# Two expert layers of a streaming encoder: x's place as a sixth weight buffer, and the shared expert's units spread over the middle blocks

## The chip, the cores and the metric

The kernel runs on one core of one Trainium2 chip. The metric is the device time of one execution in microseconds (us). Before the change the median of three runs is 1824.9 us (1823.75 to 1825.8). Times inside the kernel come from one profiled execution and are counted from its start.

## The reference

A residual trunk of two layers over 512 tokens of width 1024, all in float32. Layer 0 mixes tokens with a short gated convolution, layer 1 with gated DeltaNet linear attention. Each layer then has a mixture of experts: each token goes to the best of 8 groups and there to the best 2 of 8 experts, and a shared expert is added behind a sigmoid gate.

```python
x = x + gt1 * rmsnorm(mixer(h), norm_w[i, 1])
h = rmsnorm(x, norm_w[i, 2]) * (1.0 + sc2) + sh2
# each of 64 experts: hid = silu(xb @ w_gate[e]) * (xb @ w_up[e]); out = hid @ w_down[e]
# shared expert: ys = (silu(xt @ ws_gate) * (xt @ ws_up)) @ ws_down;  y = y + sigmoid(xt @ w_sg) * ys
x = x + gt2 * rmsnorm(y, norm_w[i, 3])
```

The residual x is 512 x 1024 words, 2 MB. Between the router's inputs and the last line nothing of the mixture of experts needs it. An expert's weights are 3 MB: 2 MB for gate and up, 1 MB for down. All 64 are loaded in each layer, 201 MB.

## The kernel before

*The ring.* All large weights go through a ring of five places in SBUF, each 128 partitions x 4096 words (2 MB). `load` (line 118) takes the next place and issues the DMA on SP's queue (lines 135 and 137). SP issues in program order: a load whose place is still being read holds up every load behind it. x has a place of its own of the same size (`new_x`).

*The blocks.* `moe` handles one layer's experts in 18 blocks, `ORDER = "QQ" + "QQPQQPQQPQQPQQQQ"`. A Q block has four experts with up to 32 tokens each, a P block two experts with up to 64. A Q block's gate and up weights take four places (`block_gu`: first the halves k < 4 of experts 0, 1 and 2, 3, then the halves k >= 4) and its down weights two (`block_dn`); a P block takes two and one. Block 0's down weights go to places outside the ring (y, hs, a `shw` buffer, part of xTb).

*One block on TensorE* (`blocks_in_order`, order written out by hand): gate-up products (line 1322, `gu`), then eight steps that alternate scatters of the block before (line 1379, `sca`, added to y by VectorE at line 1384) with gathers of a later block (line 1270, `gat`), the transposes of the hidden rows (line 1334), the down products (line 1357, `po`; for the last block line 1346, `pol`), and then, in some blocks, units of the shared expert. In the last block the scatters come ahead of the gate-up.

*The units.* Twelve per layer: eight of the shared expert's gate and up product (line 1408, `mix`), four of its down product (line 1431, `sda`). Each has a 512 KB load of its own into one of two `shw` buffers, in turn (lines 1416 and 1440). A block's unit loads are issued on SP between its gate-up and its down loads, and wait until the unit before the last has been computed. Line 1616 sets how many units a block has:

```python
n = 2 if b == NB - 2 else int(ne == 4 and not last and b > 1)
```

That is one in each of the blocks 2, 3, 5, 6, 8, 9, 11, 12, 14 and 15, and two in block 16. Behind block 16's units stands `gate_rows` (line 308, `gb`), which spreads the layer's last gate over the partitions.

*The end of a layer.* `down_last`, then `overflow`, a loop over experts with too many tokens (none here; its head at lines 1529 and 1530 is entered by all engines, and SP waits there for its loads), then the last block's scatters with the final norm and `x = x + ...` (`finish_chunk`).

*Ahead of the blocks.* `project_out` ends each mixer: per chunk of 128 tokens it adds to x (line 456), transposes x (line 544), multiplies by the router's weights (line 555) and scales x for the gathers (`front_split`, line 566). Its instructions and those of the DeltaNet mixer (`mixer1`) are put in order by a scheduler, apart from SP's.

*In `mixer1`* the decay's inputs are projected first (`project`, lines 383 to 385), transposed at line 712, worked through a chain of small VectorE instructions (lines 715 to 738, ending in `gg`), and summed by TensorE at lines 741 to 743.

Of the kernel before, what the change touches and what calls it, by code (L numbers as in the profile page):

```python
# [7 lines left out]
F32 = mybir.dt.float32  # L8
# [8 lines left out]
P = 128  # L17
T = 512
TC = T // P
D = 1024  # L20
# [18 lines left out]
ORDER = "QQ" + "QQPQQPQQPQQPQQQQ"  # L39
assert ORDER.count("P") == 4 and ORDER.count("Q") == 14  # L40
NB = len(ORDER)


def block_ranks():
# [71 lines left out]
class Trunk:  # L116
# [4 lines left out]
    def load(self, src, shape, place=None):  # L121
        n = int(np.prod(shape[1:]))
        assert n <= 4096
        if place is None:
            t = self.ring.tile([P, 4096], F32, name="ring")
        else:
            t = place.rearrange("p a b -> p (a b)")
        letters = "abcd"[:len(shape) - 1]
        v = t[:, :n]
        if len(shape) > 2:  # L130
            v = v.rearrange("p (%s) -> p %s" % (" ".join(letters), " ".join(letters)),
                            **{l: s for l, s in zip(letters, shape[1:])})
        if len(shape) == 4:
            for i in range(shape[1]):
                self.nc.sync.dma_start(out=v[:, i], in_=src[i])
        else:
            self.nc.sync.dma_start(out=v, in_=src)
        return v

    def run(self):  # L140
        nc, tc, A = self.nc, self.tc, self.A
        with tc.tile_pool(name="glob", bufs=1) as glob, \
                tc.tile_pool(name="ring", bufs=5) as ring, \
                tc.manual_schedule(engines={mybir.EngineType.SP}):
            self.glob, self.ring = glob, ring
            self.cst = glob.tile([P, C_END], F32, name="cst")
            self.ghi = glob.tile([P, K * T], F32R, name="ghi")
            self.glo = glob.tile([P, K * T], F32R, name="glo")
            self.col = glob.tile([P, W_END], F32, name="col")
            nc.scalar.dma_start(out=self.col, in_=A["cols"])  # L150
            nc.scalar.dma_start(out=self.cst, in_=A["consts"])
            self.ident = self.cst[:, C_ID:C_ID + P]
            self.new_x()
            for c in range(TC):
                nc.sync.dma_start(out=self.x[:, c], in_=A["x"][c * P:(c + 1) * P])
            self.bsu = glob.tile([P, P], BF16, name="bsu")
            nc.vector.tensor_copy(self.bsu, self.cst[:, C_SU:C_SU + P])
            self.bone = glob.tile([P, 1], BF16, name="bone")
            nc.vector.memset(self.bone, 1.0)
            tok = glob.tile([P, 2 * TC], F32, name="tok1")  # L160
            self.tok1, self.half = tok[:, :TC], tok[:, TC:]
            nc.scalar.dma_start(out=self.tok1, in_=A["tok1"])
            self.xsrc, self.xn = A["x"], None
            self.xs = tc.dram_tile([T, D], F32, name="xs")
            nc.vector.memset(self.half, -0.5)
            self.cs = glob.tile([P, K], F32, name="cs")
            nc.scalar.activation(self.cs, self.col[:, W_C:W_C + K], AF.Silu)
            self.gr = glob.tile([P, 512], F32, name="gr")
            self.mods = {}
            self.ada_tiles(0)  # L170
            self.ada_tiles(1)
            first = 0 if not self.only or min(self.only) < 2 else 1
            if self.only:
                with tc.tile_pool(name="ada0s", bufs=1) as sb, tc.tile_pool(name="ada0p", bufs=1, space=PSUM) as ps:
                    for f in self.ada_units(first, [0, 1, 2], sb, ps):
                        f()
            for n, step in enumerate((self.mixer0, lambda: self.moe(0), self.mixer1, lambda: self.moe(1))):
                if not self.only or n in self.only:
                    step()
                if self.upto == n + 1:  # L180
                    break
            if self.upto in (1, 2, 3):
                self.finish()
            self.drop_x()
# [215 lines left out]
    def project_out(self, wsrc, i, begun=None, shared=None):  # L400
# [4 lines left out]
        nc, tc = self.nc, self.tc  # L405
        front = not self.only or 2 * i + 1 in self.only
        with ExitStack() as cx:
# [41 lines left out]
            def post(c):  # L449


                parts = self.front_split(c - 1, sb) if front and c else iter(())
                next(parts, None)
                for s in halves:
                    x = self.x[:, c, s]
                    nc.vector.scalar_tensor_tensor(x, ts[c][:, s], st[c][:, 2:3], x, op0=ALU.mult, op1=ALU.add)
                    yield
                next(parts, None)
                yield
                if front:  # L460
                    yield from self.front_chunk(i, c, sb, ps)

            if shared or not begun:
                ws = w0 if shared else list(self.parts_of(w0, wp))
                for k in range(K):
                    for c in range(TC):
                        if k == 0:
                            tag, bufs = banks[0][c]
# [8 lines left out]
            for c in range(TC):  # L477
                tag, bufs = banks[1][c]
# [183 lines left out]
    def mixer1(self):  # L662
        nc, tc, A, cst = self.nc, self.tc, self.A, self.cst
# [4 lines left out]
        with ExitStack() as ctx:  # L668
            hhi, hlo = self.parts(K, T)
            with ExitStack() as cx:  # L670
# [101 lines left out]
                for h in range(H):  # L772
# [137 lines left out]
                    for j in range(4):  # L910
                        b = slice(32 * j, 32 * j + 32)
# [68 lines left out]

                if self.only:
                    wo = [self.load_out(A["gdn_out_w"], 0)]
                wo.append(self.load_out(A["gdn_out_w"], 1))
                sums = {c: ps.tile([P, T], F32, tag=("pj", "pj", "tp", "gq")[c], name="oacc", bufs=2 if c < 2 else 1)
                        for c in range(TC)}
                yhi, ylo = self.parts(TC, K, P)
                for k in range(K):
                    self.split_y(yT, [k])
                    whi = wp.tile([P, T], F32R, name="whi")
                    wlo = wp.tile([P, T], F32R, name="wlo")  # L990
                    act(whi, wo[0][:, k], AF.Copy)
                    nc.gpsimd.tensor_tensor(out=wlo, in0=wo[0][:, k], in1=r32(whi), op=ALU.subtract)
                    for c in range(TC):
                        self.mm3(sums[c], yhi[:, c, k], ylo[:, c, k], whi, wlo, k == 0, k == K - 1)
            self.project_out(A["gdn_out_w"], 1, begun=(wo, sums))

    def places(self, sb, tag, words, bufs=2):
# [447 lines left out]
    def moe(self, i):  # L1445
# [3 lines left out]
        with ExitStack() as ctx:  # L1449
# [16 lines left out]
            xA, _ = self.pair(sb)  # L1466
            xB, late = self.pair(sb)
            hw = yp[0].tile([P, D], F32, name="shw")
            src, gu = self.block_gu(i, 0, None)

            dn = self.block_dn(i, src, [self.y, hs.rearrange("p (k a) t -> p k (a t)", k=2), hw,
# [131 lines left out]
    def blocks_in_order(self, i, m, rt, rp, pairs, hs, shw, sb, ps, units, columns, scatter):  # L1603

        nc = self.nc
        xT, nxt, oh = pairs
        for b in range(1, NB):
            last = b == NB - 1  # L1610
            src, gu = self.block_gu(i, b, rt)
            ne = len(src)
            if b % 2 == 0:
                xT = nxt
            h = P * (b % 2)
            n = 2 if b == NB - 2 else int(ne == 4 and not last and b > 1)
            now = [u() for u in units[:n]]
            units = units[n:]
            dn = self.block_dn(i, src)
            adds = [(c, h) for h in range(2) for c in range(TC)]  # L1620
            if last:
                for a in adds:
                    scatter(*a)
                adds = []
            hid = self.gate_up_hid(sb, ps, [x[:, h:h + P] for x in xT], ne, gu)
            steps = iter(())
            if b < NB - 2:
                if b % 2 == 0:
                    oh = self.slot_onehot(sb, rt["slot"], P * (b + 2), 256)
                    nxt, _ = self.pair(sb)  # L1630
                steps = self.gather(ps, m, oh, nxt, (2, 3) if b % 2 else (0, 1))
            elif not last:
                steps = self.route_over(rt, rp, sb, ps)
            for n in range(8):
                if adds:
                    scatter(*adds.pop(0))
                if n == (0 if last else 5):
                    hT = self.turn(sb, ps, hid)
                next(steps, None)
            for _ in steps:  # L1640
                pass
            if not last:
                scatter = self.rows_out(sb, ps, self.down_mm(ps, hT, ne, dn), *columns(b))
            for u in now:
                u()
            if b == NB - 2:
                gt = self.gate_rows(shw, ps, 1, ("shw", "mix"))

        assert not units
        po = self.down_last(ps, hT, ne, dn)  # L1650
        self.overflow(i, m, rt, hs, sb, ps)
        if i == 0 and not self.only:
            nc.scalar.dma_start(out=hs[:, 0], in_=self.A["rows"][1])
        self.down(sb, ps, hT, ne, dn, *columns(NB - 1), self.finish_chunk(i, gt, sb, ps), False, po)
# [116 lines left out]
```

## Time and profile before

| | us |
|---|---|
| median of three runs (lowest to highest) | 1824.9 (1823.75 to 1825.8) |
| the profiled execution, its own time | 1825.65 |
| its span (first to last instruction) | 1823.8 |
| TensorE matmul busy | 1616.1 (89%) |
| VectorE busy | 852.8 (47%) |
| ScalarE busy | 479.1 (26%) |
| GpSimd busy | 175.6 (10%) |
| moved by DMA | 523.17 MB, mean 287 GB/s |

The page divides the span into 40 slices of 45.6 us and gives for each what the DMA engines moved. A busy TensorE is not one at its peak: matmuls overlap, and one that waits for its data can count as idle or run at a lower granted clock. So the stages are read one by one below: the expert blocks of layer 0 lie between 288 and 802 us, those of layer 1 between 1302 us and the end, and the DeltaNet mixer between them.

### The profile page before, as it was taken

How to read it: one execution, taken by the hardware profiler on the slowest of the kernel's cores; microseconds unless marked ns; L12 is line 12 of the kernel's file. 1: busy time of each engine (PE TensorE's matmuls, PEld its weight loads, DVE VectorE, ACT ScalarE, POOL GpSimd, SP SyncE). 2: the span in 40 equal slices, each digit the busy share in tenths (PEclk: the TensorE clock that was granted, in tenths of full speed). 3: DMA queues.
4: the chain of work that ended last, by engine and by line, in shares of the span. 5: the costliest groups of instructions: out<-in, count | busy, mean ns of one | idle time of the engine just before them, and what ended most of it. 6: DMA issues, size and time to landing. Idle time of an engine off the chain costs nothing. (4 is left out here: it accounts for less than half of the span.)

```text
span 1823.8 us, 27772 instructions
## 1 busy us (share of the span) xinstructions
PE 1616.1 (89%) x11102; PEld 985.6 (54%) x11102; DVE 852.8 (47%) x1761; ACT 479.1 (26%) x978; POOL 175.6 (10%) x160
## 2 busy tenths in 40 slices
PE   6999977899999998868998999998689999989985
PEld 3777755445445454426676766656444545445542
DVE  1886454434334342445666666625543424334335
ACT  4222351211111110034344434415231111111101
POOL 1000110000000000024323323310000000000001
PEclk8999987999999999988999999999699999999997
DMA  9873426999999999786111111116589999999992
GB/s 402 353 304 124 202 108 250 376 419 418 420 417 411 419 419 419 292 353 244 62 59 59 59 59 59 53 59 271 208 336 420 416 419 418 419 419 415 420 399 93
DMA packets 71511, 523.17 MB, mean 287 GB/s; under 512 B 8340, under 2 KB 8532, under 8 KB 16852
## 3 DMA queue, kind: packets, MB, share of 16 engines
q1 hardware_dynamic: 67684, 511.02, 68.6%
q10 hardware_dynamic: 3696, 10.34, 1.6%
q8 instruction: 89, 1.46, 0.3%
q14 instruction: 42, 0.34, 0.0%
HBM read 517.11 MB, written 4.23 MB: 286 GB/s over the span
## 5 line engine op out<-in xcount | busy, mean ns | idle before, releaser
L1384 DVE TENSOR_TENSOR y<-y,sca 128x512 f32<-128x512 f32 x272 | 186.0, 686 | 97.3 <-PE sca L1379 96.4
L1322 PE MATMUL gu<-ring,xTb 128*32 128x512 f32 (+1 forms) x1024 | 170.6, 634 | 31.8 <-DMA ring<-in_moe_gu 31.8
L1270 PE MATMUL gat<-ohg,ghi 128*128 128x256 f32 x576 | 162.6, 304 | 32.1 <-DVE ohg L1245 10.8
L1326 DVE TENSOR_TENSOR hid<-hid,gu 128x256 f32<-128x256 f32 x36 | 15.2, 421 | 311.0 <-ACT hid L1325 311.0
L1270 PE MATMUL gat<-ohg,glo 128*128 128x256 f32 x576 | 154.7, 291 | 0.0
L1270 PEld LDWEIGHTS gat<-ohg,ghi 128*128 128x128 f32 x576 | 113.8, 198 | 61.4 <-ACT xTb L1276 17.4
L1379 PE MATMUL sca<-ohi,G 128*128 128x512 f32 x288 | 126.4, 439 | 15.6 <-DVE y L1382 5.4
L1322 PE MATMUL gu<-ring,xTa 128*32 128x512 f32 (+1 forms) x1024 | 134.6, 610 | 0.2
L1322 PEld LDWEIGHTS gu<-ring,xTb 128*32 128x32 f32 (+1 forms) x1024 | 47.3, 119 | 147.1 <-issue 82.9
L1379 PE MATMUL sca<-olo,G 128*128 128x512 f32 x288 | 118.5, 411 | 0.0
L1270 PEld LDWEIGHTS gat<-ohg,glo 128*128 128x128 f32 x576 | 114.1, 198 | 7.9
L1357 PE MATMUL po<-ring,hT 128*32 128x512 f32 (+1 forms) x896 | 118.1, 602 | 0.0
L1682 POOL TENSOR_TENSOR ft<-y,gt 128x512 f32<-128x512 f32 x8 | 12.4, 1550 | 1058.9 <-DVE y L1384 1058.1
L1408 PE MATMUL mix<-h2T,shw 128*128 128x512 f32 x256 | 114.1, 599 | 0.0
L385 PE MATMUL pj<-ghi,wlo 128*128 128x512 f32 x264 | 113.4, 430 | 0.2 <-POOL wlo L681 0.2
L383 PE MATMUL pj<-ghi,whi 128*128 128x512 f32 x264 | 110.3, 418 | 1.6 <-DVE xh L789 0.8
L1325 ACT ACTIVATE hid<-gu 128x256 f32<-128x256 f32 x36 | 13.9, 385 | 357.8 <-PE gu L1322 357.8
L384 PE MATMUL pj<-glo,whi 128*128 128x512 f32 x264 | 107.8, 408 | 0.0
L681 POOL TENSOR_TENSOR wlo<-ring,whi 128x512 fp32r<-128x512 f32 x66 | 86.1, 1305 | 184.7 <-ACT whi L680 125.1
L1372 DVE SCALAR_TENSOR_TENSOR olo<-po,tab_s,ohi 128x512 fp32r<-128x512 f32 x68 | 51.1, 751 | 96.6 <-ACT ohi L1371 96.6
L1379 PEld LDWEIGHTS sca<-ohi,G 128*128 128x128 f32 x288 | 56.1, 195 | 62.8 <-issue 31.1
L1322 PEld LDWEIGHTS gu<-ring,xTa 128*32 128x32 f32 (+1 forms) x1024 | 36.6, 115 | 88.5 <-issue 88.2
(402 smaller groups left out, 2781.7 us busy)
## 6 DMA issues: line engine op xcount, KB each, us to landing
ring<-in_moe_gu SPq DMA_DIRECT2D x256, 1024.0 KB, 14.5
ring<-in_moe_w_down SPq DMA_DIRECT2D x120, 1024.0 KB, 13.2
ring<-in_ada_w SPq DMA_DIRECT2D x24, 2048.0 KB, 10.8
ring<-in_gdn_w SPq DMA_DIRECT2D x8, 2048.0 KB, 12.3
ring<-in_conv_in_w SPq DMA_DIRECT2D x8, 1536.0 KB, 11.8
shw<-in_shared_gu SPq DMA_DIRECT2D x16, 512.0 KB, 15.4
x<-in_x SPq DMA_DIRECT2D x8, 512.0 KB, 6.3
ring<-in_conv_out_w SPq DMA_DIRECT2D x2, 2048.0 KB
```

The lines of the kernel that those rows point to most:

```text
L383: mm(out, ah, bh, start=first, stop=False)
L384: mm(out, ah, bl, start=False, stop=False)
L385: mm(out, al, bh, start=False, stop=last)
L681: nc.gpsimd.tensor_tensor(out=wlo, in0=w[:, k:k + 4], in1=r32(whi), op=ALU.subtract)
L1270: nc.tensor.matmul(g[:, kk], part[:, c, k], oh[:, c], start=(kk + c + lo == 0), stop=(kk + lo == 2 and c == TC - 1), skip_group_check=True)
L1322: nc.tensor.matmul(gu[s * j:s * j + s], xT[k][:, s * j:s * j + s], pieces(j, k), start=(k == 0), stop=(k == K - 1), skip_group_check=True)
L1326: nc.vector.tensor_tensor(out=hid, in0=hid, in1=gu[:, 256:512], op=ALU.mult)
L1357: self.nc.tensor.matmul(po[h][s * j:s * j + s], hT[:, k, s * j:s * j + s], pieces(j, k)[:, 512 * h:512 * h + 512], start=(k == 0), stop=(k ...
L1372: nc.vector.scalar_tensor_tensor(lo, po[h], gcol, r32(hi), op0=ALU.mult, op1=ALU.subtract)
L1379: nc.tensor.matmul(sc, G[:, c * P:(c + 1) * P], part, start=(n == 0), stop=(n == 1))
L1384: nc.vector.tensor_tensor(out=ys, in0=ys, in1=sc, op=ALU.add)
L1408: nc.tensor.matmul(acc, w[:, k], self.h2T[:, k], start=(k == 0), stop=(k == K - 1))
```

## The change

x's residual is copied to a DRAM tile `xk` chunk by chunk as `project_out` completes it. While the blocks run, x's place stands at the end of the list of ring places, so the ring has six. After the last block's loads it leaves the list, and x is read back from `xk` on SP's queue, ahead of `down_last`. A table `UNITS` names the blocks of the twelve units: blocks 5 and 9 get two, block 16 none; `gate_rows` moves from block 16 to block 15. The ring's places are now taken from a list in place of a rotating pool; `gdn_out_w`'s second load is written behind the products that read the first.

```diff
+UNITS = (2, 3, 5, 5, 6, 8, 9, 9, 11, 12, 14, 15)
+assert all(ORDER[b] == "Q" for b in UNITS)
...
         if place is None:
-            t = self.ring.tile([P, 4096], F32, name="ring")
+            t = self.pieces.pop(0)
+            self.pieces.append(t)
...
-                tc.tile_pool(name="ring", bufs=5) as ring, \
+                tc.tile_pool(name="ring", bufs=1) as ring, \
...
+            self.pieces = [ring.tile([P, 4096], F32, name="ring%d" % n) for n in range(5)]
...
+            self.xk = tc.dram_tile([T, D], F32, name="xk")
...
+                if front:
+                    nc.scalar.dma_start(out=self.xk[c * P:(c + 1) * P], in_=self.x[:, c])
                 next(parts, None)
...
-                wo.append(self.load_out(A["gdn_out_w"], 1))
                 sums = {c: ps.tile([P, T], F32, tag=("pj", "pj", "tp", "gq")[c], name="oacc", bufs=2 if c < 2 else 1)
...
                         self.mm3(sums[c], yhi[:, c, k], ylo[:, c, k], whi, wlo, k == 0, k == K - 1)
+                wo.append(self.load_out(A["gdn_out_w"], 1))
...
+            if not self.only:
+                self.xplace = self.x.rearrange("p c d -> p (c d)")
+                self.pieces.append(self.xplace)
             src, gu = self.block_gu(i, 0, None)
...
-            n = 2 if b == NB - 2 else int(ne == 4 and not last and b > 1)
+            n = UNITS.count(b)
...
-            if b == NB - 2:
+            if b == NB - 3:
                 gt = self.gate_rows(shw, ps, 1, ("shw", "mix"))
         assert not units
+        if not self.only:
+            self.pieces = [p for p in self.pieces if p is not self.xplace]
+            for c in range(TC):
+                nc.sync.dma_start(out=self.x[:, c], in_=self.xk[c * P:(c + 1) * P])
         po = self.down_last(ps, hT, ne, dn)
```

**SP, block 16 of layer 0, before** (rows of `in_moe_gu` and `in_moe_w_down` are the ring's loads, one expert's half or a whole down matrix each):

```order
L135 ISA
L135 DMA ring<-in_moe_gu 128x2048
L1440 DMA shw<-in_shared_w_down 128x1024 x2
L135 ISA
L135 DMA ring<-in_moe_w_down 128x2048
```

**SP, block 5 of layer 0, now** (line numbers are now those of the changed kernel):

```order
L139 DMA ring_63<-in_moe_gu 128x2048
L1426 DMA shw<-in_shared_gu 128x1024 x2
L139 ISA
L139 DMA x<-in_moe_w_down 128x2048
```

The two unit loads in one block stand in block 5 (and likewise in block 9), between its gate-up and its down loads; in block 16 none stands there. x's place is written by expert loads, here a down matrix.

**SP, the end of layer 0's blocks, now:**

```order
L139 DMA ring_67<-in_moe_w_down 128x2048
L139 ISA
L139 DMA ring_67<-in_moe_w_down 128x2048
L1668 DMA x<-xk 128x1024 x4
L1543 TENSOR_LOAD oid
```

Before, the last down load was followed by the loop's head (L1529 TENSOR_LOAD oid) directly; now x's four loads stand between them.

**TensorE, the head of the DeltaNet mixer, before** (`pj` is the projection, `tp<-cst,th` the transposes of the decay's inputs, `tp<-gg,cst` the first use of the decay):

```order
L384 MATMUL pj<-glo,whi 128x512
L712 MATMUL tp<-cst,th 128x16 x4
L385 MATMUL pj<-ghi,wlo 128x512
...
L385 MATMUL pj<-ghi,wlo 128x512
L741 MATMUL tp<-gg,cst 128x32
L742 MATMUL tp<-gg,cst 128x32
L743 MATMUL tp<-gg,cst 128x32
```

**The same place now:**

```order
L393 MATMUL pj<-ghi,wlo 128x512
L722 MATMUL tp<-cst,th 128x16 x4
L391 MATMUL pj<-ghi,whi 128x512
L751 MATMUL tp<-gg,cst 128x32
L752 MATMUL tp<-gg,cst 128x32
L753 MATMUL tp<-gg,cst 128x32
```

Between the transposes and the first use stood 19 projections; now one stands there, and the others follow later.

## Rows read from the trace of the kernel before

**Rows 1.** The page's 40 slices of the span: GB/s moved in each.

```profile
GB/s 402 353 304 124 202 108 250 376 419 418 420 417 411 419 419 419 292 353 244 62 59 59 59 59 59 53 59 271 208 336 420 416 419 418 419 419 415 420 399 93
```

**Rows 2.** Windows: stretch, length, busy time by engine, clock, DMA share, GB/s.

```profile
282.00:294.00 12.00, 10.41 (x63) 6.32 (x62) 2.52 (x13) 2.04 (x4) 0.00 (x0) 0.70 0.00 1
...
322.00:761.30 439.30, 404.91 (x2348) 209.57 (x2340) 163.32 (x292) 73.42 (x137) 0.00 (x0) 0.98 1.01 416
761.30:775.50 14.20, 11.87 (x65) 4.44 (x68) 6.02 (x10) 1.20 (x2) 0.00 (x0) 1.00 0.02 10
775.50:781.50 6.00, 4.25 (x36) 1.04 (x28) 0.42 (x1) 0.77 (x2) 0.00 (x0) 1.00 0.90 350
...
1337.00:1776.50 439.50, 403.47 (x2342) 210.14 (x2334) 164.20 (x294) 73.36 (x137) 0.00 (x0) 0.98 1.01 416
```

**Rows 3.** Windows of layer 0's blocks 4 (P), 5 and 6 (Q, one unit).

```profile
405.25:424.74 19.49, 18.85 (x99) 10.32 (x99) 6.92 (x11) 2.81 (x6) 0.00 (x0) 1.00 1.01 418
424.74:451.42 26.68, 26.04 (x165) 13.67 (x163) 12.58 (x23) 5.56 (x10) 0.00 (x0) 1.00 1.02 418
451.42:484.30 32.88, 29.65 (x164) 13.56 (x163) 7.74 (x12) 4.79 (x9) 0.00 (x0) 0.95 1.01 419
```

**Rows 4.** Timeline of TensorE, block 6: start, us, instruction, idle before and releaser.

```profile
459.54 5.32 PE L1322 MATMUL gu<-ring,xTb 128*32 128x512 f32 x26 [1.46 <-DMA ring<-in_moe_gu]
...
477.23 7.13 PE L1408 MATMUL mix<-h2T,shw 128*128 128x512 f32 x16
```

**Rows 5.** Timeline of TensorE, layer 0, blocks 16 and 17.

```profile
740.13 3.64 PE L1357 MATMUL po<-ring,hT 128*32 128x512 f32 x32
743.70 3.72 PE L1431 MATMUL sda<-shw,hs 128*128 128x256 f32 x16
...
762.46 1.12 PE L308 MATMUL gb<-gr,cst 64*128 64x512 f32 x2 [0.97 <-DVE y L1435]
...
765.32 0.50 PE L1379 MATMUL sca<-ohi,G 128*128 128x512 f32 x1
...
771.11 3.64 PE L1322 MATMUL gu<-ring,xTa 128*32 128x512 f32 x32
774.57 3.62 PE L1322 MATMUL gu<-ring,xTb 128*32 128x512 f32 x32
...
782.17 3.62 PE L1346 MATMUL pol<-ring,hT 128*32 128x512 f32 x26 [0.99 <-DMA ring<-in_moe_w_down]
787.55 0.47 PE L1379 MATMUL sca<-ohi,G 128*128 128x512 f32 x1 [1.76 <-ACT ohi L1371]
```

**Rows 6.** Timeline of SP, layer 0, loads of blocks 16 and 17.

```profile
710.75 7.78 SPq L1440 DMA_DIRECT2D shw<-in_shared_w_down  x2
...
744.92 30.72 SPq L135 DMA_DIRECT2D ring<-in_moe_w_down  x4
```

**Rows 7.** Timeline of all engines, layer 0, end of project_out.

```profile
260.69 1.94 PE L544 MATMUL ftp<-cst,x 128*128 128x128 f32 x8 [4.41 <-issue]
...
262.47 3.69 PE L555 MATMUL flp<-wr,h2T 128*128 128x73 f32 x16
...
264.09 2.19 ACT L566 ACTIVATE xnf<-x,rx 128x1024 f32<-128x1024 f32 x1 [1.67 <-POOL rx L552]
```

**Rows 8.** The page's DMA issues: count, size of one, median us to landing.

```profile
ring<-in_moe_gu SPq DMA_DIRECT2D x256, 1024.0 KB, 14.5
...
xs<-x ACTq DMA_DIRECT2D x4, 512.0 KB, 13.0
x<-xs SPq DMA_DIRECT2D x4, 512.0 KB, 3.6
```

**Rows 9.** Timeline of TensorE, layer 1, first scatter behind the overflow loop.

```profile
1802.96 0.47 PE L1379 MATMUL sca<-ohi,G 128*128 128x512 f32 x1 [1.80 <-ACT ohi L1371]
```

**Rows 10.** Timeline of TensorE, head of the DeltaNet mixer.

```profile
840.04 0.42 PE L712 MATMUL tp<-cst,th 16*128 16x16 f32 x4
...
847.11 0.38 PE L741 MATMUL tp<-gg,cst 128*128 128x32 f32 x2 [2.03 <-DVE gg L738]
```

More of the change, by code (lines that the diff above doesn't have):

```diff
@@ L142, in run @@
         with tc.tile_pool(name="glob", bufs=1) as glob, \
-                tc.tile_pool(name="ring", bufs=5) as ring, \
+                tc.tile_pool(name="ring", bufs=1) as ring, \
                 tc.manual_schedule(engines={mybir.EngineType.SP}):
-            self.glob, self.ring = glob, ring
+            self.glob = glob
+            self.pieces = [ring.tile([P, 4096], F32, name="ring%d" % n) for n in range(5)]
             self.cst = glob.tile([P, C_END], F32, name="cst")
```

## The prediction

> **What bounds the kernel now.** Read first the 40 slices of the page [rows 1]: the GB/s line stands at 411 to 420 twice, in slices 9 to 16 and again from 31 to 38. These are the expert blocks of the two layers, which stream their weights. The windows of layer 0 [rows 2] show how the stretch begins and ends. The ring is full and nothing moves from 282 to 294 us (1 GB/s). From 322 to 761.3 us the DMA share is 1.01, at 416 GB/s over 439.3 us. Then it is idle again up to 775.5 (10 GB/s), and one last piece of 2.1 MB comes until 781.5. Layer 1 repeats this: 439.5 us at 416 GB/s, ending at 1776.5.
>
> So in the middle the stream is the bound, and the blocks show with how much to spare [rows 3]: the P block 4 takes TensorE 19.49 us, the Q block 5, with one unit of the shared expert, 26.68. A Q block loads twelve times 1.05 MB, 30.2 us at 416 GB/s, a P block half, 15.1, and a unit's 0.52 MB 1.3. TensorE gains on the stream in Q blocks and loses on it in P blocks; where it is ahead, it waits inside the gate-up products. Block 6 shows it [rows 4]: 1.46 us for `in_moe_gu`, and the 26 products behind that take 5.32 us. The last row is a unit: 7.13 us. A Q block without one is thus 26.68 - 7.13 = 19.55 us.
>
> The end is another matter [rows 5]. Block 16's down product begins at 740.13. Behind it stand two units of the shared expert's down product, 743.70 to 762.46 (9.4 us each), then the gate's rows to 765.32, then block 16's scatters, and only at 771.11 block 17's gate-up, whose weights ended with the stream at 761.3. One piece is missing even then: block 17's second down piece finds no free place. SP's own timeline has its four down loads begin at 744.92 and take 30.72 us to issue [rows 6]; the place comes free when half the gate-up is read, at 774.57, and the last 26 down products start at 782.17 after a 0.99 us wait for `in_moe_w_down`. The first scatter behind the overflow loop starts at 787.55. So from 761.3 on the order of work and the five places bound the kernel, not the bandwidth.
>
> **The change, part by part.** *The sixth place.* The load that before waited at 282 finds x's place and moves 2.1 MB, 5.0 us at 416 GB/s, in a stretch that was idle [rows 2]. From 294 on the four places freed by block 0 fill as before, but they now hold what comes after. The stream that starts at 322 has 2.1 MB less ahead of it, just block 17's last piece: the same 439 us now bring all weights by 761.3.
>
> *Does the place come in time?* x's last chunk is complete when its transposes start, at 260.69, and its copy to DRAM can be issued then; ScalarE's scaling reads it last, from 264.09 to 266.3 [rows 7]. The copy's landing is not in this trace; nearest is `xs<-x`, the same size and queue, 13.0 us (median) to land [rows 8]: 273.7, still before 282. Bounds: free at 266.3 or at 273.7, no cost in either. The copies' 2.1 MB lie in slices at 108 and 271 GB/s [rows 1], with room. ScalarE issues the last copy while it would wait for the transposes anyway; the order also puts the h2T copy ahead of the square, and the router's products, which end at 266.2, are later than both [rows 7]: I take 0, with ends of -0.5 and +2 for both layers.
>
> *The units.* Two down units and the gate's rows leave the end. Blocks 5 and 9 get a second unit, the others move up. Sums of TensorE against the stream, from the durations above: blocks 5 to 9, four Q, one P and six units, 4 x 19.55 + 19.49 + 6 x 7.13 = 140.5 us against 4 x 30.2 + 15.1 + 6 x 1.3 = 143.7; blocks 10 to 13, 92.3 against 93.1; blocks 14 to 16, 3 x 19.55 + 2 x 9.4 + 2.9 = 80.4 against 93.2. TensorE is faster in each, barely in the first two. So the units cost nothing as long as the ring covers the local ups and downs; six places hold 12.6 MB, 30 us of stream. If that cover is short, the stream stops. Followed load by load (5.0 us a piece; a place is free when the product that reads it ends), the tightest is block 11's second down piece, with 1 to 2 us left. So I charge 1 us per layer, with ends of 0 and 6 (nearly a unit).
>
> *The end now.* Weights end at 761.3. Before, the last piece ended near 781.4 and its products started at 782.17: 0.8 us. So the last 26 down products start at 762.1. Their time is bounded by two rows of 26 products, 3.62 us [rows 5] and 5.32 behind a wait [rows 4]. I take 5.3, since block 17 must now wait for its gate-up and its down weights: 767.4. From there to the first scatter 1.76 us, as before: 769.2. That is 787.55 - 769.2 = 18.3 us less.
>
> Here a rule speaks against the change. The rows show that products behind a short wait took 5.32 us instead of 3.62, at a granted clock that fell from 1.00 to 0.95 over the block [rows 3, 4]. The Trainium skill, page "TensorE: Matmul & The Clock Gate", section "HAM oscillation — how this bites in real kernels", says that a burst that has waited for its DMA restarts with the clock throttled, every time; by it all 26 products run at the lower of the two levels, 1.2 GHz. Twice 3.62 is 7.2 us, which makes the end 3.8 us later over two layers than the sum below; 3.62 would make it 3.4 earlier.
>
> *x comes back.* The loop behind the down products is entered by all engines, and SP, which issues the reload last, waits there for its landing. x's 2.1 MB follow the weights: 761.3 + 5.0 + 0.8 = 767.1, just under the 767.4 of TensorE. I take 0; `x<-xs`, 3.6 us for one of four [rows 8], leaves an upper end of 3 us per layer.
>
> *Layer 1*, by the same steps [rows 9]: 1776.5 + 0.8 + 5.3 + 1.8 = 1784.4 against 1802.96: 18.6 us.
>
> *What the scheduler moved.* In the DeltaNet mixer 19 projections stood between the transposes of the decay (L712) and their use (L741); now one does, as the order shows. VectorE's chain between the two lasts from 840.46 to 847.11, 6.65 us, and TensorE waited 2.03 of it [rows 10]. Now it waits 6.65 - 0.24 = 6.4, and the 18 products have to be made later: +4.4 us. Ends: 0, if TensorE would have waited later anyway; 8, if the products after the longer wait start slow. `gdn_out_w`'s second load is only written later; on SP it stands where it stood: 0.
>
> *Sum.* 18.3 + 18.6 - 2 - 4.4 = 30.5 us less than the profiled execution's 1825.65 (span 1823.8): **1795**. The median of the runs, 1824.9, lies 0.75 lower, inside the rounding here.
>
> **Rivals.**
> (a) *The ring runs full around the double units.* For it: 140.5 against 143.7 leaves 3 us in 140. Against it: the median gate-up load lands 14.5 us after its issue [rows 8], 12 of them queue. Price: 5 to 8 us per layer more, so 1805 to 1811. Chance 0.18.
> (b) *x's place comes late*, so that the sixth place does not help the fill. For it: landings of 13.0 us. Against: it would have to land 8.3 us later than that. Price: the 5.0 us per layer again, 1805. Chance 0.05.
> (c) *No slow products and no mixer stall*: 30.5 + 3.4 + 4.4, so 1787. Chance 0.10.
> (d) *All products behind block 17's waits are slow*, as the rule above has it: 7.2 us each, 1795 + 3.8 = 1799. For it: the wait of block 6 was shorter than those of block 17 will be, some 4 us. Against: block 6's 26 were slow only in part. Chance 0.12.
> (e) *SP's order turns against it: slower.* A unit's tile has two buffers, so block 6's unit load waits until block 5's first unit is done, and block 9's second until block 8's; behind them in SP's queue stand all later loads. The last places of a block's gate-up come free at its end; from there to the unit's end are 19.55 - 7.1 + 7.1 = 19.5 us (a gate-up takes 7.1, 771.11 to 778.2 [rows 5]), and the two freed places carry 10. If nothing else is queued the stream stops 9.5 us, four times over both layers: 38 us, giving 1833. For it: the same wait is there before, SP's two unit loads of block 16 begin at 710.75 and take 7.78 us [rows 6]. Against: the stream stayed at full rate through that one, and it decides only from a backlog under 9.5 us, where the rows give 12. Chance 0.05.
>
> **How the numbers follow.** My forecast, 1795, has 0.47, and 0.03 is left for a change that nets out. Faster by over 0.2% (3.6 us, about what a measurement of this kernel can tell from no change): forecast and (a) to (d), 0.92. Within it: 0.03. Slower: (e), 0.05. The range is 1786 to 1812: it takes in (c) and all of (a), the ends of the mixer and of x's reload with them, and leaves out the slower case.
>
> **What would show it.** Right: DMA share near 1 from 322 to 761 without a hole at blocks 6 and 9 to 12; about 5 us more of transfer between 282 and 294; no `sda` product in block 16; block 17's gate-up near 750, with a wait for `in_moe_gu`; the first scatter behind the loop near 769; a wait of about 6 us on `gg` in the mixer. Wrong: a hole in the stream behind a double unit, SP waiting on a unit with the DMA idle, or engines waiting for x at the loop.

## The result, and the profile after

The changed kernel takes 1794.2 us (median of four runs, 1791.25 to 1797.47) against 1825.35 before: ratio 0.9831, 95% interval 0.9813 to 0.985, 1.7% faster. The forecast was 1795. Its profiled execution is the slowest of the four, 1797.47 with a span of 1795.6.

First the page of the changed kernel: the granted clock, DMA share and GB/s of its 40 slices (44.9 us each).

```profile
PEclk8999987999999999977999999979699999999987
DMA  9874447899999999967211111108489999999995
GB/s 400 334 291 177 185 170 308 365 419 420 419 418 408 418 419 419 413 255 289 81 60 60 60 60 60 54 7 362 183 343 418 419 419 419 419 411 419 419 419 222
```

The two plateaus of [rows 1] are there, and each ends earlier. The windows of the changed kernel show their two edges and block 11 (columns as in [rows 2]):

```profile
278.00:290.00 12.00, 10.41 (x65) 6.28 (x64) 2.52 (x13) 2.04 (x4) 0.00 (x0) 0.72 0.41 170
322.00:755.00 433.00, 403.08 (x2398) 210.63 (x2397) 169.64 (x303) 75.06 (x141) 0.00 (x0) 0.99 1.01 418
755.00:762.00 7.00, 3.91 (x26) 0.90 (x30) 0.00 (x0) 0.27 (x1) 0.00 (x0) 1.00 1.00 404
...
581.66:609.46 27.80, 26.19 (x181) 15.86 (x179) 13.36 (x24) 5.57 (x10) 0.00 (x0) 1.00 0.99 403
```

The stretch that moved 1 GB/s [rows 2], here 4 us earlier, moves 170 GB/s, 2.04 MB: the sixth piece. From 322 the DMA share is 1.01 for 433 us, and only block 11 dips a little (403 GB/s). Now TensorE at the end of layer 0 (before: [rows 5]):

```profile
742.89 0.62 PE L1332 MATMUL gu<-ring,xTa 128*32 128x512 f32 x2
...
749.79 3.62 PE L1332 MATMUL gu<-ring,xTb 128*32 128x512 f32 x26 [1.45 <-DMA ring<-in_moe_gu]
...
757.27 1.04 PE L1356 MATMUL pol<-ring,hT 128*32 128x512 f32 x2 [0.89 <-DMA ring<-in_moe_w_down]
760.19 3.62 PE L1356 MATMUL pol<-ring,hT 128*32 128x512 f32 x26 [1.88 <-DMA ring<-in_moe_w_down]
766.78 0.79 PE L1389 MATMUL sca<-ohi,G 128*128 128x512 f32 x1 [2.97 <-ACT ohi L1381]
```

No unit stands behind block 16, and block 17's gate-up starts 28.2 us earlier. It waits for its weights, as do the down products: the stream is the bound up to the end. The last 26 products take 3.62 us, but the scatter waits 2.97 us where it waited 1.76 before. The DeltaNet mixer's head on TensorE (before: [rows 10]):

```profile
817.30 0.42 PE L722 MATMUL tp<-cst,th 16*128 16x16 f32 x4 [0.68 <-ACT th L719]
819.26 0.49 PE L391 MATMUL pj<-ghi,whi 128*128 128x512 f32 x1 [1.55 <-ACT whi L690]
826.46 0.61 PE L751 MATMUL tp<-gg,cst 128*128 128x32 f32 x2 [6.70 <-DVE gg L748]
...
829.43 0.80 PE L393 MATMUL pj<-ghi,wlo 128*128 128x512 f32 x1
830.02 0.63 PE L391 MATMUL pj<-ghi,whi 128*128 128x512 f32 x1
...
834.51 0.40 PE L393 MATMUL pj<-ghi,wlo 128*128 128x512 f32 x1
```

The wait is 6.70 us, and the projections behind it start every 0.43 us until 834, then every 0.23. In the kernel before, too, they start every 0.43 us behind its wait of 2.03, from 849 to 852.5.

For the sum, the span is cut at four starts of instructions on TensorE: block 0's gate-up, and the first scatter behind the loop, in both layers. All kernels of this study, in us of their profiled executions; each ratio is to the kernel before as measured beside that run on the same chip (1824.0 to 1825.6):

| kernel | to block 0 | layer 0's blocks | mixer | layer 1's blocks | tail | median, ratio to before |
|---|---|---|---|---|---|---|
| before | 288.45 | 499.1 | 515.1 | 500.3 | 20.8 | 1825.35 |
| after | 284.64 | 482.1 | 525.0 | 481.4 | 22.4 | 1794.2, 0.9831 |
| sixth_only | 283.92 | 491.3 | 529.1 | 490.0 | 20.9 | 1816.1, 0.9953 |
| units_only | 286.95 | 492.6 | 514.8 | 495.0 | 20.8 | 1811.5, 0.9937 |
| list_only | 289.92 | | 525.4 | | | 2089.4, 1.1455 (another computation, below) |
| copy_only | 284.65 | 499.5 | 514.8 | 499.1 | 21.5 | 1823.9, 1.0003 |
| units_early | 290.02 | 505.8 | 529.6 | 505.1 | 21.2 | 1843.8, 1.0089 |
| pool_ring | 289.91 | 482.6 | 508.7 | 481.2 | 22.4 | 1786.6, 0.979 |
| pool_behind | 290.07 | 482.7 | 515.6 | 480.5 | 20.8 | 1787.4, 0.9788 |
| pool_last | 285.79 | 483.7 | 514.2 | 480.3 | 21.1 | 1783.8, 0.9771 |
| after_again | 284.15 | 482.7 | 528.7 | 481.3 | 22.4 | 1798.2, 0.9847 |

The change gains 17.0 and 18.9 us in the blocks and 3.8 ahead of them, and gives back 9.9 in the mixer and 1.6 in the tail: 28.2 us of span. The block columns repeat within 1.6 us for the same blocks. The first and the mixer column don't: units_early and the changed kernel have the same code up to block 0 and differ by 5.4 us there; in the window 82 to 92 us, inside that difference, their granted clocks are 0.62 and 0.83. So only differences of 6 us or more, or rows, count in these two columns.

### The profile page after: what moved, and what is told of

It reads as the page before. It is cut to its first block, busy times and chain, and to the rows that moved or that the text cites. A ratio compares the mean times of both kernels' runs of the same rounds, so it can differ in the third digit from the quotient of the medians.

```text
span 1795.6 us, 27951 instructions
## 1 busy us (share of the span) xinstructions
PE 1602.0 (89%) x11102; PEld 985.9 (55%) x11102; DVE 853.3 (48%) x1761; ACT 478.1 (27%) x978; POOL 176.4 (10%) x160
## 4 chain that ended last, share of the span: by engine, by line
PE 67%; DMA 12%; DVE 11%; ACT 4%; issue 3%; POOL 2%; SPq 0%; ACTq 0%; POOLq 0%; DVEq 0%
PE gu L1332 11%; PE gat L1280 7%; PE po L1367 6%; PE sca L1389 6%; DMA ring<-in_moe_gu 6%; PE mix L1418 5%; PE acc L391 4%; PE acc L392 4%; PE acc L393 4%; PE sda L1441 3%; DMA ring<-in_moe_w_down 3%; PE pj L393 2%; PE pj L391 2%; PE pj L392 2%; DMA x<-xk 2%
## 5 line engine op out<-in xcount | busy, mean ns | idle before, releaser
L1332 PE MATMUL gu<-ring,xTb 128*32 128x512 f32 (+1 forms) x960 | 128.9, 607 | 9.7 <-DMA ring<-in_moe_gu 9.7
L1701 POOL TENSOR_TENSOR ft<-y,gt 128x512 f32<-128x512 f32 x8 | 12.4, 1552 | 1024.0 <-DVE y L1394 1023.2
L1332 PEld LDWEIGHTS gu<-ring,xTb 128*32 128x32 f32 (+1 forms) x960 | 36.7, 114 | 94.8 <-issue 73.3
L1418 PEld LDWEIGHTS mix<-h2T,shw 128*128 128x128 f32 x256 | 47.3, 190 | 69.7 <-issue 62.0
## 6 DMA issues: line engine op xcount, KB each, us to landing
ring<-in_ada_w SPq DMA_DIRECT2D x24, 2048.0 KB, 12.4
ring<-in_conv_in_w SPq DMA_DIRECT2D x8, 1536.0 KB, 18.9
```

Source lines behind the costliest of these rows:

```text
L1332: nc.tensor.matmul(gu[s * j:s * j + s], xT[k][:, s * j:s * j + s], pieces(j, k), start=(k == 0), stop=(k == K - 1), skip_group_check=True)
L1418: nc.tensor.matmul(acc, w[:, k], self.h2T[:, k], start=(k == 0), stop=(k == K - 1))
```

## The experiments

**The parts of the gain.** *sixth_only* is the changed kernel with the old places of the units:

```diff
-            n = UNITS.count(b)
+            n = 2 if b == NB - 2 else int(ne == 4 and not last and b > 1)
...
-            if b == NB - 3:
+            if b == NB - 2:
```

> Only the sixth place (with the copy, the reload and the list); the twelve units as before, two in block 16. Theory: every weight after block 5's down load comes 5.0 us earlier, so block 16 starts 5 us earlier, and the last piece no longer waits for block 17's gate-up (1 to 2 us more): 6 to 7 us less per layer at the first scatter behind the loop (before: 787.55), 12 to 14 in all; the list's order of the DeltaNet mixer takes 9.9 back, the front of layer 0 gives 0 to 4: 1818 to 1823. Rival: block 16's two units bind the end whatever the weights do, so the gain is only the last piece's 1 to 2 us per layer: 1830 or more.

*units_only* is the kernel before with the table and `gate_rows` in block 15, the reverse of these lines.

> Only the table of units; five places from the rotating pool, no copy of x. Theory: five places are too few for the double units in blocks 5 and 9, the stream stops there for some us and the last piece still comes late: first scatter near 779, some 8 us less per layer, total near 1810; holes in the stream in blocks 6 to 12. Rival: five places carry them too, only the 5.0 us of the last piece are missing at the end: first scatter near 772, 15 us less per layer, total near 1797; DMA share 1.0 throughout.

sixth_only: ratio 0.9953 (0.9939 to 0.9967), 7.8 and 10.3 us less in the blocks. That is more than the 6 to 7 of the theory (the total of 1816.1 lies 2 us below its 1818 to 1823) and far from the rival's 1 to 2. Its end shows what is left: the units, then all 32 down products in one run, at full clock and behind no weights.

```profile
746.54 3.72 PE L1441 MATMUL sda<-shw,hs 128*128 128x256 f32 x16 [0.97 <-DVE y L1445]
...
769.77 3.64 PE L1356 MATMUL pol<-ring,hT 128*32 128x512 f32 x32 [0.47 <-ACT hT L1346]
```

units_only: 0.9937 (0.9919 to 0.9955), 6.5 and 5.4 us less in the blocks; the total is near the 1810 of the theory (which had 8 per layer) and far from the rival's 15 and 1797. Two rows of its windows and two of its TensorE timeline say why:

```profile
569.16:588.61 19.45, 18.81 (x99) 10.28 (x98) 6.92 (x11) 2.81 (x6) 0.00 (x0) 1.00 0.83 334
588.61:616.39 27.78, 26.17 (x180) 15.86 (x178) 13.37 (x24) 5.56 (x10) 0.00 (x0) 1.00 0.95 393
```

```profile
761.85 4.13 PE L1325 MATMUL gu<-ring,xTb 128*32 128x512 f32 x32
...
772.32 5.40 PE L1349 MATMUL pol<-ring,hT 128*32 128x512 f32 x26 [0.56 <-DMA ring<-in_moe_w_down]
```

With five places blocks 10 and 11, behind block 9's two units, run the stream at shares of 0.83 and 0.95 against 1.01 elsewhere, some 5 us lost, and the last piece still waits until block 17's gate-up has freed a place at 761.85. So each part alone leaves the other's bound standing, order of work or places: the two alone add up to 14.3 and 15.7 us, together they bring 17.0 and 18.9.

**When are units hidden?** *units_early* doubles all units of the changed kernel:

```diff
-UNITS = (2, 3, 5, 5, 6, 8, 9, 9, 11, 12, 14, 15)
+UNITS = (2, 2, 3, 3, 5, 5, 6, 6, 8, 8, 9, 9)
```

> The changed kernel with all twelve units in six double ones: blocks 2, 3, 5, 6, 8 and 9. Theory: a unit is hidden only while TensorE's blocks are no longer than the loads they free; blocks 2 to 9 then take 6 x 19.55 + 2 x 19.49 + 8 x 7.13 + 4 x 9.4 = 251 us against 227 us of stream, so the ring runs full, SP waits for units with nothing queued, and the lost transfer is not made up behind it: 20 us more per layer, near 1834, with holes in the stream between 455 and 605. Rival: the layer's sum of TensorE is below the stream's, and what is lost early is won back late: 1794 to 1800.

1843.8, ratio 1.0089 (1.0062 to 1.0115): 23.6 and 23.7 us more in the blocks than after, where the theory had 20, and far from the rival's total of 1800 at most. Its windows by block (5, 8, 9 and 10) and SP's wait:

```profile
433.00:467.00 34.00, 32.67 (x182) 15.76 (x178) 12.58 (x23) 5.98 (x11) 0.00 (x0) 1.00 0.87 356
...
521.00:558.00 37.00, 33.45 (x214) 21.73 (x210) 12.31 (x23) 5.51 (x10) 0.00 (x0) 1.00 0.77 312
558.00:595.00 37.00, 33.45 (x211) 21.73 (x210) 14.58 (x29) 4.18 (x8) 0.00 (x0) 1.00 0.98 405
595.00:614.00 19.00, 18.36 (x97) 10.32 (x98) 7.11 (x12) 2.81 (x6) 0.00 (x0) 1.00 0.84 346
```

```profile
SPq L1426 <- PE mix L1418: 75.0, 8, 14.9
```

The holes are where the theory puts them, and the later blocks, stream-bound again, don't win them back. This is what rivals (a) and (e) describe, made to happen; how much of it is the full ring and how much SP's waits for units, this run doesn't separate. In the changed kernel the same row of SP reads

```profile
SPq L1426 <- PE mix L1418: 37.9, 4, 9.6
...
SPq L1544 <- DMA x<-xk: 14.8, 6, 8.7
```

The four waits of rival (e) are there, up to 9.6 us, but the queue ahead of them lasted. Block 5's stretch keeps a share of 1.01:

```profile
417.82:452.16 34.34, 33.01 (x180) 15.85 (x179) 12.58 (x23) 6.16 (x11) 0.00 (x0) 1.00 1.01 418
```

**What the mixer lost.** *list_only* is the kernel before with the list of five places in place of the pool.

```diff
-            t = self.ring.tile([P, 4096], F32, name="ring")
+            t = self.pieces.pop(0)
+            self.pieces.append(t)
```

> Only the ring's list in place of the pool, five places, with the second output load written behind the products; no copy, units as before. Theory: this alone makes the DeltaNet mixer's wait of 6.7 us and the slow projections behind it, 9.9 us more between the loop of layer 0 and block 0 of layer 1; nothing else changes: 1833 to 1836. Rival: the mixer's 9.9 come from the copies or the other changes, or the early end of layer 0: then 1825, or with the 3.8 us that layer 0's front won, 1831.

A Q block has six loads: with five fixed places its second down load takes the place of its first gate-up piece, whose products then read down weights. So its experts are another computation (the gate-up waits 252.5 us for `in_moe_w_down`), its total of 2089.4 says nothing of the 1833 to 1836 expected, and only the mixer is read from it: 525.4 us, as in the changed kernel, with a wait of 6.69 us for `gg`. Every kernel with the list has 525 to 530 us in that column, every one with the pool 509 to 516.

*copy_only* adds only the copies and the reload to the kernel before.

> Only the copy of x to DRAM and its reload ahead of the last down products; five places from the pool, units as before. Theory: the copies cost nothing, the reload follows the last piece (781.5 before) and lands some 6 to 7 us later, near 788, while the last products end at 785.8: the loop is held 1 to 3 us per layer, 1827 to 1831. Rival: the reload's landing is hidden and the front's order moves nothing: 1825; or the front gives its 3.8 us through the copy: 1822.

Ratio 1.0003 (0.9986 to 1.0021): the theory's 1827 to 1831 did not come, though its mechanism did. The mixer stays at 514.8. The loop opens 2.97 us behind the last products, as after, so the reload holds it by 1.2 us; the fronts give that back (below).

*pool_ring* keeps the pool outside the expert blocks and the list of six inside:

```diff
-            t = self.pieces.pop(0)
-            self.pieces.append(t)
+            if self.pieces is None:
+                t = self.ring.tile([P, 4096], F32, name="ring")
+            else:
+                t = self.pieces.pop(0)
+                self.pieces.append(t)
...
-                self.pieces.append(self.xplace)
+                self.pieces = [self.ring.tile([P, 4096], F32, name="ring") for n in range(5)] + [self.xplace]
```

> The change, but the ring's places come from the rotating pool outside the expert blocks, and from the list of six (five of the pool's and x's) only inside them; the second output load stands where it stood before the change. Theory: the list alone moved the projections of the DeltaNet mixer; with 19 of them back between the decay's transposes and its use, the wait falls from 6.7 to 2.0 us, the slow projections behind it go, and the 9.9 us come back: near 1784.5, the blocks as in the changed kernel. Rival: the mixer's loss comes from what the early end of layer 0 leaves behind, not from the order: 1792 to 1796.

1786.6, ratio 0.979 (0.9767 to 0.9813), near the 1784.5 of the theory. The wait at the decay's first use is again that of [rows 10]:

```profile
831.98 0.38 PE L752 MATMUL tp<-gg,cst 128*128 128x32 f32 x2 [2.03 <-DVE gg L749]
```

So the list, not the copies and not the shorter layer 0, moved the projections. (Both runs move `gdn_out_w`'s second load together with the list; which of the two edits the scheduler answered to was not separated.) The slow projections behind the wait did not go, as expected here: they start every 0.43 us up to 837.1, as in the kernel before.

**What the reload costs.** *pool_behind* reads x back behind `self.overflow(...)` in both layers, *pool_last* only in layer 1:

```diff
+        if i and not self.only:
+            for c in range(TC):
+                nc.sync.dma_start(out=self.x[:, c], in_=self.xk[c * P:(c + 1) * P])
```

> The same, and x is read back behind the loop for overflowing experts instead of ahead of the last down products. Theory: in the changed kernel the loop waits for x, which lands 5.08 us behind the last weight, while the last 26 products take 3.62: 1.2 us per layer, and the scatters behind the longer wait run at the lower clock (1.6 us in layer 1). Without it the time from the last product to the first scatter is 1.8 us again instead of 2.97, total 2.4 to 4 us less than with the reload ahead, near 1781. Rival: the reload now comes ahead of layer 1's adaLN weights, which land 5 us later, and x itself is late for the final sum: no gain, or up to 3 us more, 1784 to 1788.

There is no gain in all (0.9788, 0.9767 to 0.9809), so the theory's 1781 failed and the rival's 1784 to 1788 came. In layer 1 the scatter comes 1.74 us behind the last product in place of 2.95, and the tail is 20.8 in place of 22.4. In layer 0 the adaLN weights queue behind x: SP issues the first of them 2.2 us behind the first scatter (775.00 - 772.77), in pool_ring 1.1 us ahead of it (771.42 against 772.51). The first projection of the mixer starts 43.9 us behind that scatter (816.64 - 772.77), 41.6 in pool_ring (814.15 - 772.51). But it is 43.1 in the kernel before, without any reload, so that x's reload cost these 2.2 us is not shown.

> As with the pool outside the expert blocks, x read back ahead of the last down products in layer 0, where the adaLN weights follow it, and behind the loop in layer 1, where nothing follows. Theory: layer 1's loop opens 1.8 us behind the last product instead of 2.97, and the scatters behind it do not meet the lower clock (tail 20.8 instead of 22.4 us): 2.4 to 2.9 us less than with the reload ahead in both layers, near 1784; layer 0 as there, no late adaLN products. Rival: x, now loaded behind the loop, is late for layer 1's final sum, or the last products fall to the lower clock and end so late that the reload held nothing: 1786.6, no gain.

> The changed kernel once more, beside the one with the pool on the same chip. Both theories: near 1794. If the last 26 products of a layer run now at full clock (3.62 us), now slow (5.1 to 5.4), as the runs so far show for other kernels, the time from their start to the first scatter stays within 0.5 us, since the loop then waits for x or does not.

On one chip pool_last takes 1783.8, ratio 0.9771 (0.9748 to 0.9794), and the changed kernel 1798.2, 0.9847 (0.9822 to 0.9873): pool_last beats both. Its gain over pool_ring (0.9771 against 0.979) is within the intervals. The end of layer 1 in pool_last:

```profile
1758.47 3.62 PE L1357 MATMUL pol<-ring,hT 128*32 128x512 f32 x26 [1.43 <-DMA ring<-in_moe_w_down]
1763.89 0.47 PE L1390 MATMUL sca<-ohi,G 128*128 128x512 f32 x1 [1.80 <-ACT ohi L1382]
```

Its last 26 products take 3.62 us, so the rival's slow products did not come, and the wait is 1.80. In after_again the last 26 products of both layers took 3.62 us, with 6.48 and 6.57 us from their start to the first scatter; as none were slow, that run does not test its own expectation.

## Why the prediction was right

The total was right within 1 us, in part by luck: between the two profiled executions the gain is 28.2 us where 30.5 were forecast, the median lies 3.3 us below the profiled execution of the changed kernel, and errors of up to 5.5 us in the terms cancel in part. Its steps, one by one:

- **The sixth place**: right. The idle stretch took 2.04 MB where 2.1 were forecast. x's place was in time, as SP's rows show, with loads of `x<-in_moe_gu` issued directly behind the others, 13.7 us ahead of the 282 us of the kernel before; then SP waits for a place of the old five:

```profile
268.29 1.31 SPq L139 DMA_DIRECT2D x<-in_moe_gu  x2
289.96 1.96 SPq L139 DMA_DIRECT2D ring<-in_moe_gu  x4
```

- **The units**: right for blocks 5 to 9 and 14 to 16, which run without a hole. The sum of 92.3 us for blocks 10 to 13 is wrong: it takes 7.13 us for each of their two units, but blocks 11 and 12 now have units of the down product, priced at 9.4 elsewhere in the forecast, and with these it is 96.9, more than the stream's 93.1. These blocks took 94.6 us (562.16 to 656.75) and did not wait for the stream; the ring covered most of it. The 1 us for the ring's stalls is block 11's: 403 GB/s over 27.8 us against the 418 of the stretch is 1.0 us less transfer.
- **The end**: right in sum by two errors that cancel. The forecast from the start of the last 26 products to the first scatter was 5.3 + 1.8 = 7.1 us; it is 766.78 - 760.19 = 6.6. The products ran at full clock, 3.62, and for that very reason x's reload, priced at 0, holds the loop: SP's waits for the last weight and for x end at 760.16 and 765.24, 5.1 us apart, while the products need only 3.62. The step that failed is the comparison of 767.1 with 767.4, which took the slow products for granted. The rows of the other kernels have both halves: in pool_ring's layer 0 the products are slow and the wait is short,

```profile
765.40 5.28 PE L1357 MATMUL pol<-ring,hT 128*32 128x512 f32 x26 [1.28 <-DMA ring<-in_moe_w_down]
```

  7.1 us to the scatter at 772.51. So the total depends little on it: 6.5 to 7.5 us in the kernels whose reload directly follows the last piece. Rival (c)'s fast products came without their gain, and the 7.2 us of rival (d) came in no run: the slowest took 5.58.
- **The rule** of the Trainium skill, page "TensorE: Matmul & The Clock Gate", section "HAM oscillation — how this bites in real kernels", that a burst behind a DMA wait restarts throttled every time, is stated there of a kernel whose waits are some 3 to 5 us long. The trace does not agree for waits as short as these: behind 1.45 and 1.88 us the 26 products take 3.62 at a granted clock of 1.00. It agrees for long ones: in list_only the gate-up products behind all 22 waits of 8.9 to 16.8 us for `in_moe_w_down` start at a granted clock of 0.50. One of them:

```profile
405.35 1.89 PE L1325 MATMUL gu<-ring,xTa 128*32 128x512 f32 x2 [10.16 <-DMA ring<-in_moe_w_down]
```

- **The mixer**: the wait was right (6.4 forecast, 6.70 measured), the charge of 4.4 too small. From the first scatter to the decay's use it takes 59.7 us (826.46 - 766.78), as before (847.11 - 787.55 = 59.6), but with 25 projections made where 48 were. The step that failed is the count: besides the 18 between transposes and use, five more had moved from ahead of the transposes, and all 23 have to be made later, 23 x 0.233 = 5.4. Two terms were missing. Further on TensorE waits for `xh`, longer than before (first row):

```profile
863.10 0.51 PE L383 MATMUL pj<-ghi,whi 128*128 128x512 f32 x1 [0.80 <-DVE xh L789]
...
844.48 0.48 PE L391 MATMUL pj<-ghi,whi 128*128 128x512 f32 x1 [1.87 <-DVE xh L799]
```

  And from the use to the first `gq` product, which takes 30.1 us in place of 22.1, the granted clock is 0.87 in place of 0.92: 30.1 x 0.13 against 22.1 x 0.08, an estimated 2.1 us more lost. Together with 1.1 of the wait that is 8.6 us, for 8.0 measured. Slow products, named as the upper end of 8, are thus the smaller part. The column's 9.9 is net: 12.4 us are lost up to the transposes of layer 1's router, and 2.6 come back behind them (next point). What lies between 8.0 and 12.4 was not separated.
- **The front**: 0 was forecast, with -0.5 as the best end for both layers. From the first transposes for the router to block 0's gate-up it now takes 54.3 us in place of 56.8 in layer 0 and 53.3 in place of 55.8 in layer 1, 2.5 us less in each (1.2 to 3.0 in the other kernels with the copies). TensorE's wait at the end of `project_out` [rows 7] is gone for the most part:

```profile
256.30 1.13 PE L554 MATMUL ftp<-cst,x 128*128 128x128 f32 x8 [1.82 <-issue]
257.67 3.69 PE L565 MATMUL flp<-wr,h2T 128*128 128x73 f32 x16 [0.24 <-ACT h2T L559]
```

  4.41 us before. The router's products end at 261.36 against 266.16, with 1.35 us of that from far ahead (all products from 46 to 230 us come 1.35 to 1.39 earlier). copy_only has the same gain, so it comes with the copies, most likely from the order that they bring (the h2T copy ahead of the square), which no run changes alone; and it pays for copy_only's 1.2 us per layer. The step that failed is that the router's products were "later than both": they were late through the order.
- **Layer 1**: 17.6 net of stalls forecast, 18.9 measured, of which 1.6 goes again in the tail: behind the longer wait its first scatters take 0.77 to 0.80 us where the first took 0.47 [rows 9]. The wait does not fix the amount: in copy_only, with waits of 2.97 and 2.98 us, the tail is 21.5, between the 20.8 before and the 22.4 after.
- **`gdn_out_w`'s second load**: 0 is right, though SP issues it at 1210.24 in place of 1187.44: no engine waits for it.

So the misses in the mixer (5.5 us too little) and the tail (1.6) were paid in part by layer 0's front and start (3.8) and the blocks (1.0 more than forecast).

## What to carry to other kernels

A buffer that rests through a long stage can lend its place to the stream, if it comes free before the stream's first stall; the gain ends where the order of work behind the last weights becomes the bound. Here the place alone was worth 18 us in the blocks of both layers and the order alone 12; together they brought 36. Spread work over a stream-bound middle block by block: what counts is that TensorE falls behind the stream in no stretch by more than the ring can cover, not how the two compare over the whole. And when the way of taking buffers changes, read the order of stages that the diff doesn't touch: here a list in place of a pool, with the load moved for it, cost 10 us in a mixer that the edit does not touch.

## What the runs showed that was not expected

The same 26 products behind a short wait take 3.62 us in one execution and 5.1 to 5.6 in another, with the granted clock falling some microseconds earlier or later: 1.00 up to 764 us in the changed kernel's layer 0, and then

```profile
764.00:767.00 3.00, 0.22 (x1) 0.23 (x1) 0.73 (x2) 0.96 (x2) 0.00 (x0) 0.83 0.17 40
767.00:770.00 3.00, 1.36 (x2) 0.35 (x2) 1.86 (x3) 0.30 (x1) 0.00 (x0) 0.50 0.99 367
```

while in pool_ring's it falls ahead of the products:

```profile
760.00:763.00 3.00, 1.84 (x5) 0.32 (x6) 0.00 (x0) 0.21 (x1) 0.00 (x0) 0.83 1.02 422
763.00:766.00 3.00, 1.72 (x6) 0.20 (x8) 0.00 (x0) 0.00 (x0) 0.00 (x0) 0.50 1.00 400
766.00:771.00 5.00, 4.68 (x26) 0.93 (x18) 0.00 (x0) 0.00 (x0) 0.00 (x0) 0.72 0.42 167
```

What decides between the two was not settled. The copies of x, priced by the 13.0 us of `xs<-x` [rows 8], landed in 2.6 us (median of eight; up to 4.5 in other kernels with the copies).
